# Splits held behind both halves of the rows, 64-row logits, and the last expert finished by output halves

## The chip, the cores and the metric

The kernel runs on one core of a Trainium2 chip. The metric is the time of one execution on the device in microseconds (us); three runs of the kernel before gave a median of 2085.16 (2085.03 to 2085.52). TensorE is the matrix engine, VectorE and ScalarE are the elementwise engines, GpSimd and SyncE mainly issue transfers here; in the profile they are PE (PEld for its weight loads), DVE, ACT, POOL and SP.

## The reference, cut to what matters

256 rows of 1024 numbers in fp32 go through two blocks. The first has two layers: adaptive norm, four kinds of attention side by side ("mix"), then a feed-forward part, dense in layer 0, eight experts with the best two of them per row in layer 1; a norm ends the block. The second block has a dense feed-forward, a mix of two attentions (16 heads of 64), and another dense feed-forward, each with a norm before and after.

```python
for l in range(2):                      # first block
    x = x + g_m * (mix(adaln(x)) @ w_out[l])
    h = adaln(x)
    f = swiglu(h, ...) if l == 0 else moe_swiglu(h, router, w1, w3, w2)
    x = x + g_f * f
x = rmsnorm(x, final_norm_g)
# second block
x = x + 0.5 * rmsnorm(swiglu(rmsnorm(x, pre1), g1, g3, g2), post1)
q, k, v = split(rmsnorm(x, premix) @ w_qkv)     # s = q k^T / 8 + bias, softmax, s v
x = x + rmsnorm(norms(o) @ w_out, postmix)
x = x + 0.5 * rmsnorm(swiglu(rmsnorm(x, pre2), h1, h3, h2), post2)
```

`swiglu(h, w1, w3, w2)` is `(silu(h @ w1) * (h @ w3)) @ w2`, 2816 wide in the dense layers and 3584 in an expert.

## The kernel before, in words

The 256 rows are two tiles of 128, t=0 and t=1. Every large product is made from operands split in two: a fast 32-bit form of the number (hi, xh) and the rest (lo, xl). `mm3` (lines 213 to 217) adds three products of one tile: xh·hi, xh·lo, xl·hi. So each megabyte of weights is loaded by a transfer that SyncE issues (`wload`), cast to hi by ScalarE (line 181) and reduced to lo by VectorE (line 185), both in `wsplit`. Up to 2048 columns are split by one instruction on each engine; in the first mix it is 1024. Four staging tiles and a few pairs of hi and lo (`stp`, `spl`, with extras for each stage) bound how far this runs ahead.

The code is written as a sequence, and a planner orders the instructions of each engine from it by its own costs, in the order of the program where several are ready; each engine then runs its list in order. `behind` adds an order between two instructions of one engine without a wait. One such order is at the seams: when a norm makes the transposed operand hT for t=0 (`norm_ev`, `scaled_hT`), the splits that follow are free for 2048 columns, and those of the next 3072 stand behind t=0's last hT instructions (`hold`, HELD_FROM and HELD). For t=1 there is none. In the second block the norms are deferred: hT is made from the raw x times a column gain, and the rows' scale r comes later from square sums and a Newton root of nine small VectorE instructions (`row_rstd`, `rsqrt`).

A dense layer (`dense_ffn`) has a first block of 256 columns and five of 512. A block makes two products per row tile, w1 and w3, in two halves of the contraction (kg); `gate` (ScalarE) and `value` (VectorE) combine them; the result is transposed and multiplied by w2 into four sums (fo), which have four of the eight banks of PSUM from the start. Block 0 takes the other four, two of `pps` and two of `hps`; later blocks use the two of `pps`.

The experts (`moe_pass`) run one after another on 128 gathered rows each; an expert has seven blocks of 512 columns, two sums (eo) and the products of w2 one block late (`down`). The results of the first seven go to memory and are gathered by row: `moe_combine` issues the gathers in the last expert's block 2, and its `add` (four VectorE instructions of 1024 columns for each t) runs behind block 5 for t=0 and block 6 for t=1. The last expert's own rows are put back by products with a one-hot matrix (`scatter`): split of a sum half, two products per t, a gated multiplication and an addition to x, for one half after the other. Then, for each t, eight transposes of x and their hT pieces, the square sums, the multiplication of x by its root and the final norm's gain, and again square sums, and after that the first dense layer of the second block.

The second block's mix (`mix2`) has four groups of four heads, and for each t a unit of four heads. Keys stand in a tile with zeros so that one product of 128 rows by 512 columns gives the logits of two heads (line 1478); GpSimd clears that tile and ScalarE copies the keys of each half of the partitions (line 566).

Of the kernel before, what the change touches and what calls it, by code (L numbers as in the profile page):

```python
# [41 lines left out]
HELD_FROM = 2048  # L42
HELD = 3072
# [52 lines left out]
def kernel(ctx: ExitStack, tc: tile.TileContext, a: dict, out: bass.AP):  # L96
# [76 lines left out]
    def wsplit(ld, pool=None, pre="", late=False, after=None, into=None, at=0):  # L173
# [3 lines left out]
        step = max(n for n in (1, 2, 4) if n * w <= wide["step"])  # L177
        for k in range(0, nk, step):
# [27 lines left out]
    hold = {"ops": None, "skip": 0}  # L206
# [77 lines left out]
    def norm_ev(t, y, ps, hT, gain, shift=None):  # L284
# [15 lines left out]
        if t == 0:  # L300
            hold.update(ops=ops, skip=HELD_FROM)

    def scaled_hT(t, hT, gain):
# [10 lines left out]
        if t == 0:  # L314
            hold.update(ops=ops, skip=HELD_FROM)
# [138 lines left out]
    def dense_ffn(hT, w1, w3, w2, post, hook=None, r=None):  # L454
        with ExitStack() as es:
# [5 lines left out]
            acc = [[aps(f"fo{t}{n}") for n in range(2)] for t in range(2)]  # L461
# [13 lines left out]
            for b in range(nb + 1):  # L475
                gT = [None, None]
                if b < nb:
# [22 lines left out]
                    if b == 0:  # L500
# [69 lines left out]
    def transpose_p(ap, pt, lg, idx, nk):  # L570
        nkc = nk // T
        per_bank = 4 // nkc
        for i0 in range(0, len(idx), per_bank):
            sub = idx[i0:i0 + per_bank]
            p = hps("ptr")
            for j, i in enumerate(sub):
                for kc in range(nkc):
# [3 lines left out]
                 p[:, :len(sub) * nk].rearrange("p (a b c) -> p a b c", a=len(sub), b=nkc))  # L581

# [402 lines left out]
    def moe_turn(mp, rnd, ps, oh, tp=None, xg=None):  # L985
# [6 lines left out]
        def step(i):  # L992
# [20 lines left out]
            ohT = (tp or mp).tile([T, 256], F32R, tag="ohT", name="ohT", bufs=2)  # L1013
# [12 lines left out]
    def moe_slots(pool, posm, yd):  # L1026
        sel, gate = rt["sel"], rt["gate"]
        zero = small([T, 9], I32, name="zslot", bufs=1)
        nc.vector.memset(zero, 0)
        tab = dram.tile([T * 9, 1], I32, name="slots")  # L1030
# [4 lines left out]
        for t in range(2):  # L1035
            ok = small([T, 8], name="pok")
            nc.vector.scalar_tensor_tensor(ok, posm[t], 128.0, sel[t], op0=ALU.is_le, op1=ALU.mult)
            v = small([T, 8], name="pv")
            nc.vector.scalar_tensor_tensor(v, posm[t], 8.0, erow, op0=ALU.mult, op1=ALU.add)
            nc.vector.tensor_tensor(v, v, ok, op=ALU.mult)  # L1040
# [9 lines left out]
            none = small([T, 2], name="pnone")  # L1050
            nc.vector.tensor_scalar(none, ab, 0.0, 1025.0, op0=ALU.is_equal, op1=ALU.mult)
            put = small([T, 2], I32, name="pput")
            nc.vector.scalar_tensor_tensor(put, ab, -1.0, none, op0=ALU.add, op1=ALU.add)
            for i in range(2):
                nc.gpsimd.indirect_dma_start(tab[:, :], bass.IndirectOffsetOnAxis(ap=put[:, i:i + 1], axis=0),
                                             tok[:, t:t + 1], None)
# [41 lines left out]
    def moe_pass(mp, gp, rnd, gate, posm, yh, yl, grow, ld_fn, split_fn, first=None, yd=None):  # L1098
# [47 lines left out]
        for e in range(NE):  # L1146
            xh, xl, ohT = nxt
            acc = [aps(f"eo{n}") for n in range(2)]
            for b in range(nb):
# [50 lines left out]
                if e == NE - 1 and b >= 5:  # L1200
                    behind(add.pop(0)(), m)
# [593 lines left out]
```

## Time and profile before

| What | us |
|---|---|
| median of three runs | 2085.16 |
| profiled execution | 2086.3 |
| its span, first to last instruction | 2084.5 |
| TensorE busy in the span | 2015.6 (97%) |
| VectorE busy | 1590.2 (76%) |
| ScalarE busy | 1251.4 (60%) |

The profile is of one execution. Matmuls overlap one another, so a busy TensorE means that one is under way, and the step from one start to the next is shorter than one's duration. The granted clock is 1.00 at 2.4 GHz and 0.50 at 1.2 GHz; a stretch's number is the mean over it. A row of the waits says who waited for what: total us, times, longest.

### The profile page before, as it was taken

To read this page: it belongs to the slowest core of one execution; us is meant where nothing else is said; L and a number is where in the kernel's file an instruction comes from. 1 tells how busy PE (TensorE), PEld (TensorE's weight loads), DVE (VectorE), ACT (ScalarE), POOL (GpSimd) and SP (SyncE) were. 2 spreads that over 40 slices of the span, in tenths; PEclk is the share of its full clock that TensorE was granted. 3 is DMA by queue.
4 is the path that set the end of the run, shared out by engine and by line. 5 is a ranking of instruction groups with operands and counts; after the bars stand their busy time and mean duration, and the time that the engine had idled before them with its cause. 6 is when DMAs were issued, how large, how long until landed. Compare 5 with 4: busy or idle time off the path is not lost.

```text
span 2084.5 us, 24737 instructions
## 1 busy us (share of the span) xinstructions
PE 2015.6 (97%) x9369; PEld 1623.0 (78%) x9370; DVE 1590.2 (76%) x2044; ACT 1251.4 (60%) x1469; POOL 37.1 (2%) x37
## 2 busy tenths in 40 slices
PE   7999999999899999999999999999989999998998
PEld 3867888777678888888888888888768886777886
DVE  6897878797688888888888888888895446556544
ACT  3766434476377777777777777777654345655442
POOL 0000000000000000000000000001000000000000
PEclk9999999999899999999999999999999999999999
DMA  8846876484499999999999999999966534436530
GB/s 331 292 177 256 353 292 242 173 233 150 154 340 379 366 369 374 385 380 382 379 386 379 378 378 378 383 363 399 396 243 240 185 101 163 165 135 228 202 122 20
DMA packets 89809, 586.38 MB, mean 281 GB/s; under 512 B 12880, under 2 KB 13776, under 8 KB 23376
## 3 DMA queue, kind: packets, MB, share of 16 engines
q1 hardware_dynamic: 81184, 566.05, 72.2%
q10 hardware_dynamic: 6432, 11.84, 1.6%
q0 software_dynamic: 2064, 6.83, 0.9%
q8 instruction: 75, 1.23, 0.2%
q14 instruction: 54, 0.44, 0.1%
HBM read 578.89 MB, written 5.78 MB: 280 GB/s over the span
## 4 chain that ended last, share of the span: by engine, by line
PE 67%; DVE 3%; ACT 1%; issue 1%; DVEq 0%; ACTq 0%
PE eh L215 10%; PE eh L216 10%; PE eh L214 10%; PE eo L215 5%; PE eo L216 5%; PE eo L214 5%; PE ff L214 4%; PE ff L215 4%; PE ff L216 4%; PE fo L214 2%; PE fo L215 2%; PE fo L216 2%; DVE lo L185 1%; PE egt L1129 1%; PE pj L216 1%
## 5 line engine op out<-in xcount | busy, mean ns | idle before, releaser
L185 DVE TENSOR_TENSOR lo<-st,hi 128x2048 fp32r<-128x2048 f32 (+2 forms) x327 | 648.1, 2002 | 138.2 <-ACT hi L181 131.2
L181 ACT CAST hi<-st 128x2048 fp32r<-128x2048 f32 (+2 forms) x328 | 540.2, 1681 | 156.9 <-PE ff L216 58.7
L185 DVE TENSOR_TENSOR lo<-sx,hi 128x2048 fp32r<-128x2048 f32 (+1 forms) x200 | 451.8, 2274 | 131.5 <-ACT hi L181 128.8
L181 ACT CAST hi<-sx 128x2048 fp32r<-128x2048 f32 (+1 forms) x200 | 374.5, 1899 | 136.5 <-PE ff L216 97.0
L214 PE MATMUL eh<-hi,xeh 128*128 128x512 f32 x896 | 351.4, 392 | 8.2 <-PEq L1415 5.1
L215 PE MATMUL eh<-lo,xeh 128*128 128x512 f32 x896 | 353.3, 394 | 2.4 <-DVE lo L185 2.4
L216 PE MATMUL eh<-hi,xel 128*128 128x512 f32 x896 | 350.4, 391 | 0.0
L214 PE MATMUL ff<-hi,hTh 128*128 128x512 f32 (+1 forms) x576 | 221.6, 385 | 10.5 <-DVE hTl L312 4.6
L215 PE MATMUL ff<-lo,hTh 128*128 128x512 f32 (+1 forms) x576 | 217.1, 377 | 1.5 <-DVE lo L185 1.5
L216 PE MATMUL ff<-hi,hTl 128*128 128x512 f32 (+1 forms) x576 | 217.4, 378 | 0.1
L214 PEld LDWEIGHTS eh<-hi,xeh 128*128 128x128 f32 x896 | 169.1, 189 | 45.2 <-ACTq L1415 5.5
L215 PEld LDWEIGHTS eh<-lo,xeh 128*128 128x128 f32 x896 | 169.2, 189 | 41.3 <-DVE lo L185 7.1
L216 PEld LDWEIGHTS eh<-hi,xel 128*128 128x128 f32 x896 | 169.2, 189 | 34.5
L215 PE MATMUL eo<-lo,egh 128*128 128x512 f32 x448 | 179.7, 401 | 0.3 <-DVE lo L185 0.3
L214 PE MATMUL eo<-hi,egh 128*128 128x512 f32 x448 | 175.2, 391 | 0.7 <-ACT egh L220 0.7
L216 PE MATMUL eo<-hi,egl 128*128 128x512 f32 x448 | 174.9, 390 | 0.5 <-DVE egl L220 0.5
L214 PEld LDWEIGHTS ff<-hi,hTh 128*128 128x128 f32 x576 | 111.5, 194 | 29.9 <-DVE hTl L312 4.8
L214 PE MATMUL pj<-hi,hTh 128*128 128x512 f32 (+3 forms) x320 | 123.9, 388 | 4.2 <-ACT hTh L220 3.1
L215 PEld LDWEIGHTS ff<-lo,hTh 128*128 128x128 f32 x576 | 111.5, 194 | 20.0 <-DVE lo L185 2.0
L216 PEld LDWEIGHTS ff<-hi,hTl 128*128 128x128 f32 x576 | 111.2, 193 | 20.1 <-DVE hTl L220 0.4
L216 PE MATMUL pj<-hi,hTl 128*128 128x512 f32 (+3 forms) x320 | 122.7, 384 | 3.4 <-DVE hTl L220 1.9
L215 PE MATMUL pj<-lo,hTh 128*128 128x512 f32 (+3 forms) x320 | 125.1, 391 | 0.9 <-DVE lo L185 0.8
(383 smaller groups left out, 2611.3 us busy)
## 6 DMA issues: line engine op xcount, KB each, us to landing
st<-in_e_dram SPq DMA_DIRECT2D x192, 1024.0 KB, 7.4
sx<-in_e_dram SPq DMA_DIRECT2D x144, 1024.0 KB, 7.6
st<-in_ada_dram SPq DMA_DIRECT2D x30, 1024.0 KB, 5.1
sx<-in_g_dram SPq DMA_DIRECT2D x19, 1024.0 KB, 6.0
sx<-in_h_dram SPq DMA_DIRECT2D x19, 1024.0 KB, 4.9
sx<-in_ada_dram SPq DMA_DIRECT2D x18, 1024.0 KB, 10.3
st<-in_w_in_dram SPq DMA_DIRECT2D x16, 1024.0 KB, 5.0
sx<-in_f_dram SPq DMA_DIRECT2D x15, 1024.0 KB, 7.0
```

Source lines behind the costliest of these rows:

```text
L181: c = nc.scalar.copy(hi[:, d], st[:, s])
L185: d = nc.vector.tensor_tensor(*rest.pop(), op=ALU.subtract)
L214: m = nc.tensor.matmul(ps, xh, wh, start=start, stop=False)
L215: nc.tensor.matmul(ps, xh, wl, start=False, stop=False)
L216: nc.tensor.matmul(ps, xl, wh, start=False, stop=stop)
L1129: nc.tensor.transpose(p[:, j * T:(j + 1) * T], g[:, j * T:(j + 1) * T], ident)
```

## The change

- `hold` becomes a list with a range for each t: splits whose first column counts 2048 to 5120 since t=0's hT stand behind t=0's last hT instructions, and those from 4096 to 8192 behind t=1's. Splits below 4096 have pieces of at most 1024 columns, and in `mix2` all have.
- `mix2` makes logits from keys without zeros: `row_logits` issues four products of 64 rows by 256 columns for a unit, on partitions 0 to 63 and 64 to 127 in turn, into two banks.
- The last expert ends with `finish_last`: products of sum half 0 for the last two blocks, then those of half 1, with half 0's split, scatter and additions (`back(0)`) before the last of these; `back(1)` is returned and called later. Its one-hot matrix is kept in another pool. The combine's adds stand behind blocks 4 and 5.
- The first dense layer of the second block gets a `start`: its block 0 runs by contraction halves, with four products' sums in the four banks `aps` (the fo sums take them afterwards). `start(h)` makes the hT pieces of half h for both t; `start(0)` then calls `back(1)`; both take square sums of x, multiply x by the final gain, and take square sums again; `start(2)` makes both roots for both t at once, and scales x.
- `moe_slots` uses a table of 16 instead of 9 numbers per partition, and drops the instruction that sent unused entries past its end.

```diff
-HELD_FROM = 2048
-HELD = 3072
+HELD = ((2048, 5120), (4096, 8192))
+FINE = 4096
...
-        step = max(n for n in (1, 2, 4) if n * w <= wide["step"])
+        step = max(n for n in (1, 2, 4) if n * w <= (1024 if hold["n"] < FINE else wide["step"]))
...
-            if hold["ops"] is not None:
-                if hold["skip"] <= 0:
-                    behind(c, hold["ops"][0])
-                    behind(d, hold["ops"][1])
-                hold["skip"] -= min(step, nk) * w
-                if hold["skip"] < -HELD:
-                    hold["ops"] = None
+            for first, last, ops in hold["ops"]:
+                if first <= hold["n"] < last:
+                    behind(c, ops[0])
+                    behind(d, ops[1])
+            hold["n"] += min(step, nk) * w
...
+    def scaled_half(t, h, hT, gain):
+        p = hps("trx")
+        for j in range(4):
+            nc.tensor.transpose(p[:, j * T:(j + 1) * T], halves(x[t])[h][:, j * T:(j + 1) * T], ident)
+        for j in range(4):
+            c, src = 4 * h + j, p[:, j * T:(j + 1) * T]
+            g = gain[:, c:c + 1]
+            nc.scalar.activation(hT[t][0][:, c, :], src, AF.Copy, scale=g)
+            nc.vector.scalar_tensor_tensor(hT[t][1][:, c, :], src, g, hT[t][0][:, c, :].bitcast(F32),
+                                           op0=ALU.mult, op1=ALU.subtract)
...
+                    if b == 0 and start is not None:
+                        lds = {(wi, kg): wload("f1", flat, kg) for kg in range(2) for wi, flat in enumerate((w1, w3))}
+                        p = {(t, wi): aps(f"ff{wi}{t}") for t in range(2) for wi in range(2)}
+                        for kg in range(2):
+                            start(kg)
+                            hl = pair()
+                            ws = [wsplit(lds[wi, kg], into=hl, at=wi * 4 * w) for wi in range(2)]
+                            for t in range(2):
+                                for wi in range(2):
+                                    up(p[t, wi], t, kg, ws[wi])
+                        start(2)
+                        for t in range(2):
+                            gate(t, p[t, 0])
+                            value(t, p[t, 1])
+                        acc = [[aps(f"fo{t}{n}") for n in range(2)] for t in range(2)]
...
+    def row_logits(bank, t, nk, qT, kT):
+        p = []
+
+        def f(h):
+            if not p:
+                p.extend(bank(f"lgr{i}") for i in range(2))
+                for k in range(4):
+                    hp, i = divmod(k, 2)
+                    r = slice(i * 64, (i + 1) * 64)
+                    nc.tensor.matmul(p[i][:, hp * nk:(hp + 1) * nk], qT[r, hp, t * T:(t + 1) * T],
+                                     kT[r, hp, :nk], start=True, stop=True)
+            hp, i = divmod(h, 2)
+            return p[i][:, hp * nk:(hp + 1) * nk]
+        return f
...
+        def finish_last(acc, ohT, gT, g):
+            def products(n, b, g):
+                ws = split_fn(ld_fn("e2", "e2", 2 * b + n, NE - 1))
+                for k in range(4):
+                    mm3(acc[n], g[0][:, k * T:(k + 1) * T], g[1][:, k * T:(k + 1) * T], *ws[k],
+                        False, b == nb - 1 and k == 3)
+
+            def back(n):
+                sl = slice(n * 512, n * 512 + 512)
+                e = wk.tile([T, D], F32R, tag="y", name="eys", bufs=2)
+                split_to(halves(e)[0], halves(e)[1], acc[n])
+                for t in range(2):
+                    p = (pps if n else hps)("sct")
+                    for i in range(2):
+                        nc.tensor.matmul(p, ohT[:, t * T:(t + 1) * T], halves(e)[i], start=i == 0, stop=i == 1)
+                    nc.vector.scalar_tensor_tensor(p, p, gate[t][:, NE - 1:NE], grow[:, sl], op0=ALU.mult, op1=ALU.mult)
+                    nc.vector.tensor_tensor(x[t][:, sl], p, x[t][:, sl], op=ALU.add)
+
+            products(0, nb - 2, gT)
+            g = transposes(g)
+            products(0, nb - 1, g)
+            products(1, nb - 2, gT)
+            back(0)
+            products(1, nb - 1, g)
+            return lambda: back(1)
...
-                if e == NE - 1 and b >= 5:
+                if e == NE - 1 and b >= 4:
                     behind(add.pop(0)(), m)
...
-            widen(ap, MIX_PAIRS[1])
+            widen(ap, MIX_PAIRS[1], 1024)
...
-                kb = ap.tile([T, 2, 2, 256], F32, tag="k2", name="k2", bufs=2)
-                nc.gpsimd.memset(kb, 0.0)
+                kb = ap.tile([T, 2, 256], F32, tag="k2", name="k2", bufs=2)
...
-                    for g in range(2):
-                        evac(kb[g * 64:(g + 1) * 64, :, g, t * T:(t + 1) * T], p4[g * 64:(g + 1) * 64, 2:4, :])
+                    evac(kb[:, :, t * T:(t + 1) * T], p4[:, 2:4, :])
...
-    for t in range(2):
-        scaled_hT(t, hT, fgain)
-        r = row_rstd(t, "x")
-        for n in range(2):
-            xs = halves(x[t])[n]
-            nc.vector.scalar_tensor_tensor(xs, xs, r, halves(fin)[n], op0=ALU.mult, op1=ALU.mult)
-        q = row_rstd(t, "q")
-        nc.vector.tensor_tensor(q, q, r, op=ALU.mult)
-        r1.append(q)
+    def start1(h):
+        if h < 2:
+            for t in range(2):
+                scaled_half(t, h, hT, fgain)
+            if h == 0:
+                rest()
+            for t in range(2):
+                xs = halves(x[t])[h]
+                for i in range(2):
+                    if i:
+                        nc.vector.tensor_tensor(xs, xs, halves(fin)[h], op=ALU.mult)
+                    jk = wk.tile([T, 512], BF16, tag="junk", name="junk", bufs=2)
+                    nc.scalar.activation(jk, xs, AF.Square, accum_out=fsum[:, 2 * i + h, t:t + 1])
+            return
...
+        for t in range(2):
+            r1.append(s[10][:, t:t + 1])
+            nc.vector.tensor_scalar(x[t], x[t], s[5][:, t:t + 1], None, op0=ALU.mult)
```

## Rows read from the trace of the kernel before

**Rows 1.** The page's first part: busy us, share of the span, instructions.
```profile
PE 2015.6 (97%) x9369; PEld 1623.0 (78%) x9370; DVE 1590.2 (76%) x2044; ACT 1251.4 (60%) x1469; POOL 37.1 (2%) x37
```
**Rows 2.** Busy time by stretch: PE, PEld, DVE, ACT, POOL, clock, DMA share, GB/s.
```profile
700.00:1430.00 730.00, 730.00 (x3316) 601.10 (x3315) 639.53 (x357) 531.29 (x372) 9.20 (x5) 1.00 0.98 378
1480.00:1500.00 20.00, 20.00 (x92) 16.55 (x91) 17.04 (x10) 15.22 (x11) 0.00 (x0) 1.00 1.00 406
1500.00:1520.00 20.00, 17.57 (x77) 13.71 (x76) 19.09 (x13) 11.68 (x9) 0.00 (x0) 1.00 0.77 269
1520.00:1562.00 42.00, 33.11 (x172) 27.07 (x171) 38.42 (x80) 23.74 (x45) 0.00 (x0) 0.88 0.67 252
1735.00:1757.00 22.00, 17.72 (x73) 12.51 (x71) 18.78 (x53) 16.67 (x33) 0.00 (x0) 0.92 0.56 203
1757.00:1880.00 123.00, 121.88 (x622) 94.72 (x621) 66.74 (x161) 72.21 (x160) 1.90 (x2) 1.00 0.47 165
1878.00:1903.00 25.00, 19.27 (x120) 17.42 (x119) 18.95 (x53) 18.32 (x35) 0.00 (x0) 0.86 0.58 231
```
**Rows 3.** Who TensorE waited for: us in total, times, longest.
```profile
PE ff L214 <- DVE hTl L312: 4.6, 1, 4.6
...
PE ff L214 <- ACT hTh L220: 3.1, 1, 3.1
...
PE eh L215 <- DVE lo L185: 2.4, 3, 1.8
PE ff L214 <- ACT s L483: 2.3, 1, 2.3
...
PE sct L1112 <- DVE x L1116: 2.0, 1, 2.0
...
PE trx L307 <- DVE x L1116: 1.7, 1, 1.7
PE pj L216 <- DVE hTl L312: 1.6, 1, 1.6
...
PE sct L1112 <- ACT eyh L220: 0.7, 1, 0.7
```
**Rows 4.** Busy time of the combine's (DVE, POOL) and the scatter's (PE, PEld, DVE) instructions.
```profile
1499.00:1530.00 31.00, 8.93 (x8) 0.00 (x0) 1.00 0.59 204
...
1530.00:1542.00 12.00, 3.63 (x8) 1.65 (x8) 5.21 (x8) 0.82 0.57 201
```
**Rows 5.** The last dense layer's start in order of time, then a stretch (as rows 2).
```profile
1887.49 2.29 DVE L185 TENSOR_TENSOR lo<-sx,hi 128x2048 fp32r<-128x2048 f32 x1
...
1890.20 2.29 DVE L185 TENSOR_TENSOR lo<-sx,hi 128x2048 fp32r<-128x2048 f32 x1
...
1893.19 0.61 DVE L312 SCALAR_TENSOR_TENSOR hTl<-trx,cols,hTh 128x128 fp32r<-128x128 f32 x2 [0.18 <-ACT hTh L311]
...
1896.09 0.15 DVE L246 SCALAR_TENSOR_TENSOR rsq<-rsq 128x1 f32<-128x1 f32 x1
...
1897.42 0.16 DVE L238 SCALAR_TENSOR_TENSOR rsq<-rsq 128x1 f32<-128x1 f32 x1
...
1893.59:1899.50 5.91, 5.91 (x27) 5.91 (x28) 3.26 (x20) 4.41 (x12) 0.00 (x0) 0.50 0.67 277
```
**Rows 6.** The second mixing layer's start in order of time, VectorE and ScalarE.
```profile
1743.26 2.29 DVE L185 TENSOR_TENSOR lo<-st,hi 128x2048 fp32r<-128x2048 f32 x1
...
1749.01 2.28 DVE L185 TENSOR_TENSOR lo<-st,hi 128x2048 fp32r<-128x2048 f32 x1
...
1756.35 0.68 ACT L1463 ACTIVATE n<-pj,rsk 128x512 f32<-128x512 f32 x1
```
**Rows 7.** Logits: the group of line 1478, then two of line 675 by time.
```profile
L1478 PE MATMUL lg<-k,q 128*128 128x512 f32 x32 | 15.6, 608 | 0.4 <-ACT k L566 0.3
...
152.06 1.02 PE L675 MATMUL lgp<-kbc,qTc 128*128 128x512 f32 x2
...
140.41 1.10 PE L675 MATMUL lgp<-kbc,qTc 128*128 128x256 f32 x4
```

More of the change, by code (lines that the diff above doesn't have):

```diff
@@ L460, in dense_ffn @@
             es.callback(stages, None)
-            acc = [[aps(f"fo{t}{n}") for n in range(2)] for t in range(2)]
+            if start is None:
+                acc = [[aps(f"fo{t}{n}") for n in range(2)] for t in range(2)]
             nb = len(FF_BLOCKS)
@@ L1027, in moe_slots @@
         sel, gate = rt["sel"], rt["gate"]
-        zero = small([T, 9], I32, name="zslot", bufs=1)
+        zero = small([T, 2 * NE], I32, name="zslot", bufs=1)
         nc.vector.memset(zero, 0)
-        tab = dram.tile([T * 9, 1], I32, name="slots")
+        tab = dram.tile([T * 2 * NE, 1], I32, name="slots")
         nc.gpsimd.dma_start(tab.rearrange("(p f) o -> p (f o)", p=T), zero)
@@ L1049, in moe_slots @@
             ab = two("pab")
[L1050 to L1051 removed]
             put = small([T, 2], I32, name="pput")
[L1053 removed]
+            nc.vector.tensor_scalar(put, ab, -1.0, 0.0, op0=ALU.add, op1=ALU.max)
             for i in range(2):
@@ L1056, in moe_slots @@
                                              tok[:, t:t + 1], None)
+            ok = small([T, 8], name="pok")
+            nc.vector.scalar_tensor_tensor(ok, posm[t], 128.0, sel[t], op0=ALU.is_le, op1=ALU.mult)
             nc.vector.tensor_tensor(ok, ok, enot, op=ALU.mult)
@@ L1170, in moe_pass @@
                         nc.vector.tensor_tensor(g, s, p, op=ALU.mult)
+                if rnd == 0 and e == NE - 1 and b == nb - 1:
+                    return finish_last(acc, ohT, gT, g)
                 if prev is not None:
@@ L1432, in moe @@
                 widen(mp, MOE_PAIRS)
-                moe_pass(mp, mo, 0, gate, posm, yh, yl, grow, load,
+                rest = moe_pass(mp, mo, 0, gate, posm, yh, yl, grow, load,
                          lambda ld: ld if isinstance(ld, list) else wsplit(ld, after=end.pop() and (rt["mm"], rt["mm"]) if end else None),
@@ L1437, in moe @@
                 widen()
+        return rest
     def mix2(hT, r, then):
@@ L1589 @@
             if not t:
[L1590 removed]
+                begin["op"] = hold["ops"][0][2][0]
     def chain(*fs):
@@ L1631 @@
     mix1(1, h_m1[0], feed([(1, 3), router_setup, (1, 5)], MIX1_ADA), lambda t, acc: rt.update(acc=acc) if t else route0(acc))
-    moe()
+    rest = moe()
     fin = load_row(ROW_FIN)
@@ L1649, with root @@
     hT, r1 = hT_tiles(), []
-    for t in range(2):
-        scaled_hT(t, hT, fgain)
-        r = row_rstd(t, "x")
-        for n in range(2):
-            xs = halves(x[t])[n]
-            nc.vector.scalar_tensor_tensor(xs, xs, r, halves(fin)[n], op0=ALU.mult, op1=ALU.mult)
-        q = row_rstd(t, "q")
-        nc.vector.tensor_tensor(q, q, r, op=ALU.mult)
-        r1.append(q)
+    fsum = sml.tile([T, 12, 2], F32, name="fsum")
+    def start1(h):
[12 more added lines that the diff above has]
+            return
+        s = [fsum[:, i, :] for i in range(12)]
+        tt = nc.vector.tensor_tensor
+        def root(v, r):
+            nc.vector.tensor_scalar(v, v, D * EPS, None, op0=ALU.add)
+            rsqrt(v, s[6], s[7], s[8], r, math.sqrt(D))
+        tt(s[4], s[0], s[1], op=ALU.add)
+        root(s[4], s[5])
+        tt(s[9], s[2], s[3], op=ALU.add)
+        tt(s[9], s[9], s[5], op=ALU.mult)
+        tt(s[9], s[9], s[5], op=ALU.mult)
+        root(s[9], s[10])
+        tt(s[10], s[10], s[5], op=ALU.mult)
+        for t in range(2):
+            r1.append(s[10][:, t:t + 1])
+            nc.vector.tensor_scalar(x[t], x[t], s[5][:, t:t + 1], None, op0=ALU.mult)
     norm_mx, h_mx, r_mx = deferred(col("premix"), "k")
     norm_f2, h_f2, r_f2 = deferred(col("pre2"), "q")
-    dense_ffn(hT, a["g1"], a["g3"], a["g2"], chain(normed_residual(load_row(ROW_P1), 0.5), norm_mx), r=r1)
+    dense_ffn(hT, a["g1"], a["g3"], a["g2"], chain(normed_residual(load_row(ROW_P1), 0.5), norm_mx), r=r1, start=start1)
     mix2(h_mx, r_mx, norm_f2)
```

39 lines of the change are left out of this document (16 added, 23 removed).

## The prediction

> **What bounds the kernel now.** I read the page's first part, then busy time by stretch, then who TensorE waited for, then the instructions in order of time at the places where it waited. TensorE is busy 2015.6 of 2084.5 us [rows 1]: only its own work or its idle time can shorten the run, and other engines count where TensorE waits for them. By stretch [rows 2], the experts' middle has TensorE busy all of its 730 us at full clock (730 / 3316 records = 0.22 us each), and the second mixing layer 121.9 of 123; there only less TensorE work counts. The losses stand at seams: 1500 to 1562 (the last expert into the next dense layer) has 62.0 - 17.57 - 33.11 = 11.3 us idle, and a mean granted clock of 0.88 in its longer part; 1735 to 1757 (into the second mixing layer) 4.3 us idle at 0.92; 1878 to 1903 (into the last dense layer) 5.7 us at 0.86. At the first, VectorE is nearly full: 19.09 of 20 and 38.42 of 42. The waits [rows 3] name the same places: 4.6 for a late hTl at the last seam and 1.6 at the one before, 2.4 for lo beside the combine, 2.0 and 1.7 for x at the scatter, 2.3 for a gate's s.
>
> **Last dense layer (orders).** The second half of the rows (t=1) has its hTl pieces between two splits of the next weight block: VectorE runs lo of 2.29 us at 1887.49 and again at 1890.20, and the last pair of hTl starts at 1893.19; TensorE takes up at 1893.59, and then makes 27 records in 5.91 us at a granted clock of 0.50 [rows 5]. The change puts the splits of elements 4096 to 8192 behind t=1's last piece. Both 2.29 leave the chain: hTl is done 4.6 earlier, near 1889.2, about when t=0's products end (the wait of 4.6 before 1893.59 began at 1889.0). So the 4.6 goes, and if the clock stays up, half of the 5.91 (3.0) too: 7.6. What is late next: rsq, done at 1897.58, comes at 1893.0, and TensorE, 48 products of 256 columns later (0.11 each, 5.3 us), wants the next block at about 1894.5; its moved split of 2.29 can follow rsq, at 1895.3 or somewhat later. I take 7.6 less 1.1 for that wait and 1.5 for a clock that still dips: **-5**, bounds -8 and 0 (the splits are wanted at once, and the wait only moves).
>
> **Second mixing layer (orders and finer splits).** The same pattern: lo of 2.29 at 1743.26, for which TensorE waits, and another at 1749.01 ahead of t=1's last hTl [rows 6]. In pieces of 1024 the first can start TensorE 1.1 us sooner; the other leaves the chain (2.3). The limit behind it is the row scale: the first product's evacuation waits for it until 1756.35, and as its squares follow the last hTh it comes 2.3 sooner too, a little more with the 1.1. **-3**, bounds -6 (the idle time of the stretch and its slow clock) and 0. Cutting this layer's 16 splits in two costs one more start each on engines that are busy 66.74 and 72.21 of 123 us [rows 2]: nothing.
>
> At the other seams the same orders bring nothing: there TensorE waits 3.1 for t=0's hTh [rows 3], which no weight split stands ahead of in either version. The slot table's arithmetic precedes a gather wanted only by the next expert: nothing.
>
> **Row products.** 16 products of 128 rows by 512 columns are 32 records [rows 7]. Two in a row of such a form take 1.02 us, and the last of them some 0.6 (the mean of one is 608 ns), so one begins per 0.43: 32 x 0.43 = 13.8 us. The new form has 32 products of 64 rows by 256 columns, 64 records; one of 256 columns costs half, 0.215, or by the row of four, of which the last takes some 0.4, (1.10 - 0.4) / 3 = 0.23. One after another: 64 x 0.215 = 13.8, or 14.9. Whether two halves of the rows overlap no row shows. If they pair wholly, half: -6.9. The records of every row start in order, so in a unit of four products the second record of one could run with the first of the next: five steps instead of eight, 8 units x 5 x 0.215 = 8.6, -5.2. A switch between 128 and 64 rows drains at worst what a record takes beyond its step, 0.6 - 0.43 = 0.17, 16 times: +2.7. Bounds -6.9 and +1.1 + 2.7 = +3.8. I take -5.2 with two thirds of the drains: **-3.5**. TensorE is full in this layer, so this reaches the end undiminished. One copy of k less, and one memset less, stand on engines with room: nothing.
> The Trainium skill's TensorEngine Tiling (Array Packing), section Key Properties, says that tiles of the array load weights and multiply in parallel, but that a change of tiling mode drains TensorE. No run here shows either yet; by its first half alone the term would be -5.2, by its second up to 2.7 less.
>
> **Experts' end into the dense layer.** Before, the combine (8.93 us of VectorE in 31 [rows 4]) runs in the last two blocks on a full engine. TensorE waits 2.4 for lo, 0.7 for the scatter's first split, 2.0 and 1.7 for x, 2.3 for s [rows 3]. The change moves each half of the combine a block earlier: its first half, 4.47, goes into a stretch where VectorE had 20 - 17.04 = 2.96 free [rows 2], so 1.5 spills and may stall TensorE by up to the 2.4 that it costs now. The sum's half 0 is finished first: its scatter, adds and transposes of half of x lie beside 12 or 24 products of half 1 (2.6 or 5.3 us), and half 1's chain beside the first half of block 0, 48 products of 256 columns (5.3). A half's chain: split 1.3, products 3.63 / 2 = 1.8, gated adds 5.21 / 2 = 2.6 [rows 4], eight transposes, counted as 256-column products, 0.9, and a first pair of hT pieces 0.6 [rows 5]: 7.2. So 1.9 stays open twice, 3.8. The gates then wait for both roots, some 28 small steps in a row after the last square; nine took 1.5 us (1896.09 to 1897.58 [rows 5]), so 4.7. Block 0 sits in the sums' four banks, so 24 products of the next block in the other two (5.3) cover that, and the 2.3 for s goes.
> Waits gone: 0.7 + 2.0 + 1.7 + 2.3 = 6.7, less the 3.8 that stay open: 2.9. The clock: 0.12 of 42 us is 5.0 lost, 4.0 of it while busy; with idle times of 2 instead of a row of them I count it as won: **-6.5** (rounded down from 6.9).
> VectorE's own limit: the norm gain and root take four operations of 512 columns and two of 1024 where four did both, at most 4 x 0.65 = 2.6 more. It could win its idle 0.91 + 3.58, the 4.47 moved out and one split not yet due, 2.3, less 2.6: 8.7, so -6.5 fits. Bounds -11 (all idle time) and +5 (the spilled combine stalls 2.4 more and the 2.6 is all late).
>
> **Sum.** -5 - 3 - 3.5 - 6.5 = -18. The profiled execution took 2086.3 us (span 2084.5 and 1.8 around it), so 2068.3; it lies 1.1 above the median of the runs, 2085.16, which makes **2067.2**.
>
> **The rivals.**
> *A. Row products do not overlap and drain.* For: no row shows an overlap, and records start in order. Against: the halves use other rows and other banks. +3.8 for -3.5: 2074.5. Chance 0.17.
> *B. The waits at the two later seams move.* The held splits come late, after squares on ScalarE and roots on VectorE. For: TensorE needs the next split and a bank freed by a row scale. Against: both come 2.3 to 4.6 earlier than before. Those two terms are nothing: 2075.2. Chance 0.12.
> *C. All goes well.* No seam has a slow clock and the rows pair wholly: 7 more, 2060. Chance 0.07.
> *D. The other side: VectorE's queue at the experts' end.* It was busy 57.5 of 62 us there; two chains now follow one another, with more work. If it lags at the first, TensorE idles before block 0 and again at its second half, and the lag carries the held splits of the later seams' pattern into this one: +5, and +2.7 for the drains without a gain from rows, nothing at the other seams: some 2093. It decides from where VectorE has no gap up to the first 512-column product of that dense layer and TensorE idles there over 11 us. Chance 0.05.
> *E. It does not do what it says*: the instructions' planned order stays, the moved adds trade places: 2085. Chance 0.04.
>
> **How the numbers follow.** The forecast, 2061 to 2073, has 0.55; the rest is above. A to C lie in 2058 to 2079, which is the range: it leaves out D, E and the tails of B and C, under 0.2. Within 0.2% (4.2 us) is about what a measurement here cannot tell from no change. Faster 0.88 (the forecast, C, nearly all of A and B), the same 0.06 (E, tails of B), slower 0.06 (D, tails of A).
>
> **What would show it.** Right: lo stalls in the blocks with the combine, but no wait of over 2 us at the scatter or for s; TensorE's wait for hTl at the last seam under 1 us, and that layer's first 512-column product some 5 us nearer to its start; 64-row records that start in pairs, their mean step well under 0.2 us. Wrong: 64-row records 0.215 or more apart; a granted clock below 0.9 still at all three seams; VectorE without a gap from 1483 to the dense layer.

## The result and the profile after

The changed kernel takes 2065.44 us (median of 4 runs, 2063.29 to 2069.5) where the one before took 2085.34 beside it: a ratio of 0.9904, 95% interval 0.9887 to 0.9921, or 19.9 us. The forecast was 2067.2. The profiled execution took 2065.45 with a span of 2063.7.

The page's first part, of after (busy us, share of the span, instructions), against [rows 1]:

```profile
PE 2002.4 (97%) x9402; PEld 1616.4 (78%) x9402; DVE 1589.7 (77%) x2049; ACT 1251.0 (61%) x1477; POOL 36.2 (2%) x33
```

TensorE is busy 13.2 us less, of 20.8 us of span: the larger part of the gain is busy time (half clock and the row products), the rest idle time. Busy time by stretch, of after, against [rows 2] (columns as there):

```profile
700.00:1430.00 730.00, 730.00 (x3316) 601.07 (x3315) 639.62 (x357) 531.45 (x372) 9.21 (x5) 1.00 0.98 378
1480.00:1500.00 20.00, 17.56 (x77) 13.65 (x77) 18.72 (x12) 11.68 (x9) 0.00 (x0) 1.00 0.90 349
1500.00:1520.00 20.00, 18.04 (x80) 14.23 (x79) 19.25 (x13) 14.29 (x10) 0.00 (x0) 1.00 0.83 304
1520.00:1557.00 37.00, 34.74 (x205) 30.17 (x204) 34.66 (x51) 24.95 (x45) 0.00 (x0) 1.00 0.69 276
1557.00:1575.00 18.00, 15.55 (x70) 12.49 (x69) 10.45 (x30) 8.55 (x10) 0.00 (x0) 1.00 0.89 370
1728.00:1750.00 22.00, 20.36 (x96) 15.49 (x95) 18.50 (x55) 17.14 (x39) 0.00 (x0) 1.00 0.41 130
1750.00:1866.00 116.00, 115.20 (x637) 92.66 (x635) 68.53 (x176) 70.68 (x163) 0.00 (x0) 1.00 0.53 189
1863.00:1881.00 18.00, 16.56 (x116) 14.39 (x115) 15.12 (x50) 14.52 (x33) 0.00 (x0) 1.00 0.59 231
```

The granted clock is 1.00 at all three seams, where it was 0.88, 0.92 and 0.86. New is the second row: TensorE, full from 1480 to 1500 before, now stands still for 2.4 us there. The waits of after, against [rows 3] (us, times, longest):

```profile
PE eh L218 <- DVE lo L185: 4.0, 3, 1.8
...
PE ff L217 <- ACT hTh L223: 3.1, 1, 3.1
PE pj L217 <- ACT hTh L223: 3.1, 1, 3.1
PE ff L217 <- ACT s L496: 2.5, 1, 2.5
...
PE trx L320 <- DVE x L461: 1.9, 3, 1.5
...
PE ff L219 <- DVE hTl L313: 1.8, 2, 1.2
...
PE ff L217 <- DVE hTl L325: 0.3, 1, 0.3
```

The 4.6 for hTl is 0.3, the scatter's waits are gone, the two of 3.1 are as before; lo has grown from 2.4 to 4.0, and the 2.3 for s, which I said would go, is 2.5.

Where the time went is best seen between fixed points of TensorE's work. The table has the distances between starts of its records, read from each trace: first expert product to the last sum of the dense layer behind the experts; from there to the last o product (the second mixing layer); from there to the last 256-column product of the last dense layer (the last seam); from there to the last product of w2 (the rest). In the same table is the ratio to the kernel before with its interval.

```
kernel                       experts+dense   mix2   seam   rest   ratio [95%]
before                          1168.42     141.55  22.55  174.46
after                           1162.02     133.27  15.85  174.93  0.9904 [0.9887, 0.9921]
e1 rows alone                   1168.36     138.90  22.33  174.46  0.9995 [0.9986, 1.0004]
e2 orders alone                 1165.84     136.46  15.84  174.91  0.9935 [0.9922, 0.9949]
e3 no orders                    1161.02     138.95  22.51  174.46  0.9958 [0.9944, 0.9971]
e4 rows in other order          1162.03     134.09  15.83  174.97  0.9908 [0.9893, 0.9923]
e5 whole splits                 1161.68     135.44  15.84  174.95  0.9912 [0.9890, 0.9935]
e6 combine spread               1161.51     133.27  15.84  174.95  0.9906 [0.9889, 0.9922]
e7 roots first                  1159.70     133.16  15.84  174.91  0.9896 [0.9879, 0.9912]
e8 both                         1158.37     133.47  15.84  174.92  0.9884 [0.9867, 0.9900]
e9 pieces, no hold for t=1      1161.23     138.05  21.42  174.46  0.9941 [0.9921, 0.9961]
e10 combine partly on ScalarE   1158.11     133.48  15.85  174.92  0.9874 [0.9854, 0.9894]
e11 half the combine left out   1161.41     133.64  15.85  174.95  0.9898 [0.9877, 0.9918]
e12 combine partly on GpSimd    1160.99     133.54  15.83  174.91  0.9883 [0.9863, 0.9903]
```

What lies ahead of the first expert product is not in it: it ends anywhere from 565.7 to 570.8 us in these traces, without order. Seam and rest repeat within 0.2 us in kernels that do not differ there, mix2 within some 0.5 (133.2 to 133.6 in after, e6 to e8 and e10 to e12). The first column holds the first expert, which takes from 120.6 to 122.0 us, also without order (its waits for hi are 3.1 in before's list, 4.3 in after's, 2.7 and 4.2 in e3's and e2's). Counted from the second expert's first product, the column repeats much better: 1047.6 in before and e1; 1044.1 in e2; 1040.3 to 1040.6 in after, e3, e4, e5, e6, e9 and e11; 1038.1 in e7; 1036.5 in e8; 1037.1 in e10; 1039.0 in e12. Small effects are read from these distances; the ratios alone would not show them.

### The profile page after: what moved, and what is told of

The parts are those of the page before. It is cut to its first block, busy times and chain, and to the rows that moved or that the text cites. A ratio compares the mean times of both kernels' runs of the same rounds, so it can differ in the third digit from the quotient of the medians.

```text
span 2063.7 us, 24799 instructions
## 1 busy us (share of the span) xinstructions
PE 2002.4 (97%) x9402; PEld 1616.4 (78%) x9402; DVE 1589.7 (77%) x2049; ACT 1251.0 (61%) x1477; POOL 36.2 (2%) x33
## 4 chain that ended last, share of the span: by engine, by line
PE 68%; DVE 2%; ACT 1%; issue 1%; DMA 1%; SPq 0%; DVEq 0%; ACTq 0%
PE eh L218 10%; PE eh L219 10%; PE eh L217 10%; PE eo L218 5%; PE eo L217 5%; PE eo L219 5%; PE ff L219 4%; PE ff L218 4%; PE ff L217 4%; PE fo L217 2%; PE fo L218 2%; PE fo L219 2%; DVE lo L185 1%; PE egt L1171 1%; PE pj L218 1%; PE pj L219 1%
## 5 line engine op out<-in xcount | busy, mean ns | idle before, releaser
L219 PE MATMUL ff<-hi,hTl 128*128 128x512 f32 (+1 forms) x576 | 212.7, 374 | 2.3 <-DVE hTl L313 1.8
```

Of the source, the lines that this page charges most:

```text
L219: nc.tensor.matmul(ps, xl, wh, start=False, stop=stop)
```

## The experiments

**Each part alone.** e1 has of the change only `row_logits`, with its tile of keys; e2 only the two held ranges and the pieces of 1024; e3 is after without these (the main lines):

```diff
-HELD = ((2048, 5120), (4096, 8192))
+HELD_FROM = 2048
+HELD = 3072                        # t=0 alone, as before
-        step = max(n for n in (1, 2, 4) if n * w <= (1024 if hold["n"] < FINE else wide["step"]))
+        step = max(n for n in (1, 2, 4) if n * w <= wide["step"])
-            widen(ap, MIX_PAIRS[1], 1024)
+            widen(ap, MIX_PAIRS[1])
```

> The kernel before with the row products alone. Theory (whole pairing, a price at each switch): in the trace of after the 64-row records start in pairs 0.006 to 0.007 us apart, a pair every 0.209 us, so four steps a unit, and each switch costs about 0.3 us (0.1 on the record before, 0.1 on the first pair, 0.1 at the exit); summed from start to start its records take 10.2 us where the 128-row form took 13.5. So -3.3 us against before, and all of it between the first pj product and the last o product of the second mixing layer. Rival (my prediction's working): five steps of eight and two thirds of sixteen drains of 0.17 us, -3.5, which is the same sum by another split: told apart by the pair step and the record before a switch, not by the time. Rival A (no overlap, drains): +3.8. The total alone can't tell -3.3 from nothing with certainty; the stretch in the trace can.

Measured: -2.65 in the second mixing layer and nothing elsewhere; the time, 2083.35, is not told apart from before, as expected of so small a part. The -2.65 is not the products' price alone. Summed from start to start, their records take 9.3 us where they took 13.5. The half clock at that seam (0.92 over 22 us before, 1.8 us lost) is gone too, and in its place TensorE waits for n; before's list has no such wait. The stretch of [rows 2], of e1, and the wait:

```profile
1735.00:1757.00 22.00, 16.45 (x70) 11.56 (x69) 19.16 (x50) 17.54 (x31) 0.00 (x0) 1.00 0.56 204
```
```profile
PE pj L214 <- ACT n L1478: 1.4, 1, 1.4
```

> The kernel before with the two held ranges and the 1024-element splits alone. Theory: the orders give what the traces of before and after show at the two later seams: last o product to the last 256-column product of the last dense layer 22.5 us before, 15.8 in after, -6.7; and first pj to last o of the second mixing layer -8.3 in after, less 3.3 for the rows, -5.0; together -11.7, a time near 2073.6. The prediction had -8 (2077). Rival: part of the second mixing layer's gain came from how the dense layer before it ended in after (its shortened experts' end), so the orders alone give -6.7 and about -3 there: 2075.6. Rival B (waits move): no change, 2085.

Measured: 2070.69. The last seam gives -6.7 and the mixing layer -5.1, as the theory had it. Unforeseen, the dense layer behind the experts gains too, in its old form: experts+dense is 2.6 shorter (3.5 behind the last expert, less the first expert's wait), and e2's list of waits no longer has the 2.3 for s, while the mean clock from 1520 to 1562 is 0.92 where it was 0.88 (1.7 us). The "other seams" of my prediction are not nothing.

> The kernel after with the orders and the finer splits undone: rows and the experts' end remain. Theory (the parts add): 3.3 for the rows and 6.4 for the experts' end with its dense layer (first expert product to the last sum of that dense layer is 6.4 us shorter in after than in before): -9.7, a time near 2075.6, with half-clock stretches back at the two later seams. Rival (the parts lean on each other): the dense layer's start in block 0 needs its held splits, so without the orders the experts' end gives 3 or less: 2079 or more.

Measured: 2075.74, the theory's time. The half clock is back at the last seam only (0.86 from 1867 to 1892); at the one into the second mixing layer it is 1.00, as in e1. Against e1 (rows alone) the experts' end gives -7.3. Against e2, where the orders have already won at that place, the same code gives only -3.8: the parts do not add there.

**What pairs the row products.** e4 issues the two products of the lower rows first, then the two of the upper:

```diff
-                for k in range(4):
+                for k in (0, 2, 1, 3):
```

> The kernel after with the four 64-row products of a unit in another order: both of the lower 64 rows first, then both of the upper ones. Theory (records start in order, and only a record that stands right behind one of the other half can run beside it): eight records of a unit take seven steps instead of four, 3 x 0.209 x 8 units = 5.0 us more than after. Rival (the halves queue independently, each record starts when its rows are free): the four of the lower half run beside the four of the upper one, no change against after.

Measured: next to no loss (2065.94; mix2 +0.8, not +5.0). TensorE's rows by time, of after and then of e4 (start, us, what, count; the stretch of a group is that of all its records):

```profile
1758.10 0.40 PE L217 MATMUL pj<-hi,hTh 128*128 128x512 f32 x1
1758.44 0.49 PE L620 MATMUL lgr<-k,q 64*128 64x256 f32 x2
...
1758.44 2.00 PE L620 MATMUL lgr<-k,q 64*128 64x256 f32 x16
1760.36 0.50 PE L218 MATMUL pj<-lo,hTh 128*128 128x512 f32 x1
```
```profile
1758.72 0.40 PE L217 MATMUL pj<-hi,hTh 128*128 128x512 f32 x1
1759.06 0.49 PE L620 MATMUL lgr<-k,q 64*128 64x256 f32 x2
...
1759.06 2.10 PE L620 MATMUL lgr<-k,q 64*128 64x256 f32 x16
1761.09 0.49 PE L218 MATMUL pj<-lo,hTh 128*128 128x512 f32 x1
```

The second line of each, a look at the first 0.02 us, has two records under way within 0.49 us, and one alone takes 0.48: they run side by side. In after 16 records, two units, fill 1.92 us up to the next product; at one per 0.215 they would fill 3.4. In e4 the program has two records of each of two products of the lower half ahead of any of the upper, and they pair nevertheless, 2.03 us for 16. So the halves take their records independently in both orders that were run, and my rule that records of all rows start in order falls. The Trainium skill, TensorEngine Tiling (Array Packing), section Key Properties, says that tiles operate independently: this trace agrees.

**The pieces and the hold.** e5 takes the pieces of 1024 out (the last two pairs of lines of e3's diff); e9 keeps them and holds nothing behind t=1:

```diff
-        hold["ops"].append((*HELD[t], ops))
+        if t == 0:
+            hold["ops"].append((*HELD[0], ops))
```

> The kernel after with whole splits (2048 elements) again, the two held ranges stay. Theory (my prediction's working): in the second mixing layer the pieces of 1024 start TensorE 1.1 us sooner and the hold of t=1 brings the rest, so first pj to last o grows from 133.3 to 134.4 us, the last seam (15.85 us from the last o to the last 256-column product) stays, and the run is 1.1 longer. Rival 1 (the pieces carry the seam): they account for the gain beyond my 3 us there (5.1 to 5.7 measured), so that stretch grows by 2 or more. Rival 2 (the pieces are idle): no change there, and the 0.45 us that the rest of the last dense layer took longer in every kernel with the orders goes.

> The kernel after with the second held range (t=1's) taken out: the pieces of 1024 and t=0's range stay. Theory (my prediction's step for the last seam, and what the run with whole splits left over at the other): all of the gain from the last o to the last 256-column product, 6.7 us, is that range's, so 15.85 goes back to 22.5; and of the 5.7 us of the second mixing layer the pieces have 2.2, so first pj to last o grows from 133.3 by the remaining 3.5: in all some 10 us slower than after. Rival: the pieces alone already let t=1's hTl through between two halves of a split, so part of the gain stays, some 3 us at each of the two places.

Measured: without the pieces mix2 is 2.2 longer, with waits for lo (1.5) and for a late lg (1.1) in e5's list, so rival 1 holds; the seam does not need them. Without the hold both places fall back, mix2 by 4.8 and the seam by 5.6 of its 6.7, and its wait is there again (waits of e9):

```profile
PE ff L218 <- DVE hTl L326: 4.6, 1, 4.6
...
PE pj L218 <- ACT n L1535: 2.4, 1, 2.4
```

Against e3, which has neither, the hold alone is worth 138.95 - 135.44 = 3.5 in mix2, the pieces alone 138.95 - 138.05 = 0.9, not much above the scatter of that column, and both 5.7. Alone the pieces bring TensorE earlier to a late root (the 2.4 for n, 1.4 in e3's list), and behind that wait stands half clock, which e3 has not there (e9):

```profile
1735.00:1757.00 22.00, 18.98 (x75) 14.41 (x75) 16.05 (x38) 15.25 (x28) 0.00 (x0) 0.92 0.73 263
```

That is 22 x 0.08 = 1.8 us of what the pieces win beside the hold. At the seam they keep 1.1 of the gain without the hold, with the same wait of 4.6 as in e3 and a clock of 0.93 (1866 to 1891) for 0.86. The hold costs 0.47 in the rest of the last dense layer: the moved split is not yet there when TensorE starts the next block at 1880.23, and its first product with lo starts 0.54 behind the one before it, where 0.23 is usual (after):

```profile
1878.42 2.29 DVE L185 TENSOR_TENSOR lo<-sx,hi 128x2048 fp32r<-128x2048 f32 x1
```
```profile
1880.23 0.49 PE L217 MATMUL ff<-hi,hTh 128*128 128x512 f32 x1
1880.77 0.50 PE L218 MATMUL ff<-lo,hTh 128*128 128x512 f32 x1
```

I had allowed 1.1 for that wait.

**The two waits that after has and I had not forecast.** The combine on VectorE, of after, in its first block (by time):

```profile
1488.08 2.29 DVE L185 TENSOR_TENSOR lo<-st,hi 128x2048 fp32r<-128x2048 f32 x1
1490.28 1.22 DVE L1135 TENSOR_TENSOR ycomb<-ycomb,row 128x1024 f32<-128x1024 f32 x1
1491.41 0.69 DVE L223 TENSOR_TENSOR egl<-egt,egh 128x512 fp32r<-128x512 f32 x1
1492.01 1.22 DVE L1136 TENSOR_TENSOR x<-x,ycomb 128x1024 f32<-128x1024 f32 x1
1493.14 6.69 DVE L185 TENSOR_TENSOR lo<-st,hi 128x2048 fp32r<-128x2048 f32 x3
...
1557.89 0.16 DVE L1735 TENSOR_TENSOR fsum<-fsum 128x2 f32<-128x2 f32 x1
1557.96 0.75 DVE L1741 TENSOR_SCALAR x<-x,fsum 128x1024 f32<-128x1024 f32 x1
1558.63 0.15 DVE L1736 TENSOR_TENSOR fsum<-fsum 128x2 f32<-128x2 f32 x1
1558.70 0.75 DVE L1741 TENSOR_SCALAR x<-x,fsum 128x1024 f32<-128x1024 f32 x1
1559.36 0.16 DVE L1729 TENSOR_SCALAR fsum<-fsum 128x2 f32<-128x2 f32 x1
1559.43 2.28 DVE L185 TENSOR_TENSOR lo<-sx,hi 128x2048 fp32r<-128x2048 f32 x1
1561.63 0.16 DVE L226 TENSOR_SCALAR fsum<-fsum 128x2 int32<-128x2 int32 x1
1561.70 1.22 DVE L185 TENSOR_TENSOR lo<-sx,hi 128x1024 fp32r<-128x1024 f32 x1
1562.84 0.15 DVE L232 TENSOR_TENSOR fsum<-fsum 128x2 f32<-128x2 f32 x1
...
1564.20 0.16 DVE L1738 TENSOR_TENSOR fsum<-fsum 128x2 f32<-128x2 f32 x1
```

Above, VectorE goes from one thing to the next without a gap, and the split at 1493.14 is the one TensorE waits for (the step between its records is 1.97 longer than the usual 0.22 there, and 1.99 longer in the next block). Below are the roots: small steps (fsum), and between two of them whatever large piece was ready. The chain takes from 1553.58 to 1564.36.

e6 puts the combine's eight operations one behind each half block of blocks 3 to 6; e7 puts the w3 splits of the second block and the scaling of x behind the roots; e8 has both.

```diff
 # e6
-                if e == NE - 1 and b >= 4:
-                    behind(add.pop(0)(), m)         # four operations at once
+                    if rnd == 0 and e == NE - 1 and b >= 3:   # in the loop over e1, e3
+                        behind(add.pop(0)(), m)     # one operation
 # e7
+            if rooted is not None:                  # in wsplit; b == 1, w3
+                behind(d, rooted)
-            nc.vector.tensor_scalar(x[t], x[t], s[5][:, t:t + 1], None, op0=ALU.mult)
+            behind(nc.vector.tensor_scalar(x[t], x[t], s[5][:, t:t + 1], None, op0=ALU.mult), end)
```

> The kernel after with the combine's eight VectorE operations one behind each half block of the last expert's blocks 3 to 6, instead of four behind each of blocks 4 and 5. Theory (VectorE's queue): four operations of 4.47 us in one block of 16.8 us overrun the 2 to 3 us that VectorE has free in a block, so lo comes late and TensorE waits 2.9 us in the first such block and 2.3 in the second; two operations of 2.2 us a block fit, and 4 of these 5.2 us go: first to last expert product from 953.7 to some 950, the run 3 to 4 us shorter. Rival (the stall belongs to the gathered rows or the shared memory, not to the queue): the waits for lo stay near 4 us in sum wherever the operations stand. A second rival: the last two operations, now in block 6, make x late for the first scatter and add as much at the experts' end.

Measured: the theory and its second rival both. From the first to the last product of the experts' first two matrices it is 4.2 shorter (953.72 to 949.56; 3.5 from the second expert on), and from there to the dense layer's end 3.65 longer. 1.9 of that is a new wait for lo in block 6 (1.7 idle, and the longer step of the record ahead); the rest is clock, in a stretch behind the wait for s (e6):

```profile
PE eo L218 <- DVE lo L185: 3.6, 4, 1.7
...
PE ff L217 <- ACT s L496: 2.5, 1, 2.5
```
```profile
1560.00:1575.00 15.00, 12.55 (x51) 9.87 (x50) 6.00 (x13) 5.69 (x8) 0.00 (x0) 0.89 0.64 267
```

The same wait of 2.5 is followed by full clock in after, 1.00 over the same 15 us, and here by a mean of 0.89: 15 x 0.11 = 1.65.

> The kernel after with the small steps of both roots ahead of the second block's w3 splits and of the scaling of x. Theory (VectorE's queue again): in after the roots' chain runs from 1553.58 to 1564.3 us with 2.2, 2.28 and 1.22 us of splits and 1.34 us of scaling of x between its steps, while TensorE can do only the 48 products of the second block's first matrix until the gates free its banks; with the splits behind, the roots end near 1557.5, the gates free the banks before TensorE asks, and its wait of 2.6 us for s at 1563.4 goes: last expert product to the end of that dense layer from 208.3 to 205.7 us. Rival (the wait moves): the w3 splits, 2.29 us each and now behind roots, scaling and gates, are late by as much; 208 stays, with a wait for lo in place of that for s.

Measured: as the theory had it. The chain runs from 1552.82 to 1557.26 and no wait for s is in e7's list; -2.3. VectorE, of e7, at its end:

```profile
1556.90 0.16 DVE L243 SCALAR_TENSOR_TENSOR fsum<-fsum 128x2 f32<-128x2 f32 x1
1557.10 0.16 DVE L1741 TENSOR_TENSOR fsum<-fsum 128x2 f32<-128x2 f32 x1
1557.18 1.41 DVE L1744 TENSOR_SCALAR x<-x,fsum 128x1024 f32<-128x1024 f32 x2
```

> The kernel after with both: the combine's operations spread and the roots' steps first. If both theories hold and add, 3.5 + 2.6 = 6 us less than after, near 2059. If they share a cause later on (the scatter or x late), less than the larger of the two gains is added by the other.

Measured: -3.65 in experts+dense, 2061.04 us. With the wait for s gone the clock stays up (1.00 from 1550 to 1575), and the spread combine is worth 1.6 from the second expert on (1038.1 to 1036.5); the 1.9 in block 6 remains.

e10 to e12 change the combine again, e10 and e12 on top of e7:

```diff
 # e10: first operation of a half; the other six behind the half blocks of blocks 3 to 5
-            f = nc.vector.tensor_scalar(g[0], g[0], w[:, 0:1], None, op0=ALU.mult)
+                nc.scalar.activation(g[0], g[0], AF.Copy, scale=w[:, 0:1])
 # e11
-                if e == NE - 1 and b >= 4:
+                if e == NE - 1 and b >= 5:
 # e12: as e10 but for the places of the operations, and
-            nc.vector.tensor_tensor(g[0], g[0], grow, op=ALU.mult)
+                nc.gpsimd.tensor_tensor(g[0], g[0], grow, op=ALU.mult)
```

> The kernel after with the roots' steps first, the combine's first operation of each half of the rows on ScalarE, and its other six on VectorE, one behind each half block of the last expert's blocks 3 to 5, so that none is left in block 6. Theory (VectorE's queue, and block 6 has no room since its own chain ends there): the wait of 1.9 us in block 6, which came with two operations there, goes, and those of 0.8 stay: first expert product to the end of that dense layer from 1159.7 us (roots first alone; 1158.4 with eight operations over four blocks) to some 1156.5. Rival (2.5 us of VectorE a block is too much for the 2.4 it has free): waits for lo of 2 us come back in blocks 4 and 5, and it stays at 1158 or more.

Measured: 1158.11, no better than e8, and 0.6 longer than it from the second expert on. In block 6 a wait of 0.6 is left of the 1.9, and two of 0.7 stayed, much as expected; but ScalarE's scaling now delays a split's other half (waits of e10):

```profile
PE eo L220 <- DVE lo L185: 2.1, 3, 0.7
...
PE eo L219 <- ACT hi L181: 1.3, 1, 1.3
```

> The kernel after with the combine's two halves back behind blocks 5 and 6 of the last expert, where the kernel before has them; all else as after. Theory (block 6 has no room): the second half's 4.47 us of VectorE now runs among the split of the sum and the first scatter; x is late for the first row transposes, and what the experts' stretch wins (2.3 of its waits) comes back larger after it: first expert product to the end of that dense layer from 1162.0 to 1164 or more. Rival (only the number of full blocks counts): the stall has the same size in whichever block, 1162.0 within 0.7.

In this form the last block returns ahead of the line that issues its operations, so the second half of the combine (t=1) is left out, and the question is not answered. What it tells: the half that is left stalls TensorE as before (a gap of 1.97 in its block), and experts+dense is no shorter than after's from the second expert on (1040.3 for 1040.4), because what is won (2.6) ahead of the wait for s is lost behind it to a stretch at 0.89, as in e6. Whether the combine belongs in the late blocks stays open.

> The kernel after with the roots' steps first, and the combine on three engines: the first scaling on ScalarE, the product with the output row on GpSimd, and only two operations a half (1.28 and 1.22 us) on VectorE, one behind a half block of blocks 3 to 5. Theory (VectorE's queue alone makes the stalls): VectorE has 1.28, 2.5 and 1.22 us of the combine in three blocks that have some 2.4 free each, so the waits for lo shrink to those that stand there anyway (0.7 and 0.8 at the experts' end): first expert product to the end of that dense layer from 1158.1 us (the best so far) to some 1156, and the run 1 to 3 us under it. Rival (the two engines block each other): a GpSimd operation that reads two tensors of SBUF holds up the splits on VectorE, which read two as well; then splits of 2.29 us stand in the trace with over 3 us beside the GpSimd operation, lo is late there, and the stretch stays at 1158 or grows by what the GpSimd operations last. The rule for the rival is in the Trainium skill, SBUF — State Buffer, section SBUF: two separate sides: the pair of ports that VectorE and GpSimd share is a lock for a whole instruction.

Measured: 1160.99, 2.9 worse than e10, of which 1.0 is the first expert's and 1.9 the last one's; the rival holds. GpSimd and VectorE by time, and the waits, of e12:

```profile
1463.69 2.41 POOL L1137 TENSOR_TENSOR ycomb<-ycomb,row 128x1024 f32<-128x1024 f32 x1 [19.48 <-DVE ycomb L1136]
...
1483.32 4.38 POOL L1137 TENSOR_TENSOR ycomb<-ycomb,row 128x1024 f32<-128x1024 f32 x1 [17.22 <-DVE ycomb L1136]
...
1485.36 4.50 DVE L185 TENSOR_TENSOR lo<-sx,hi 128x2048 fp32r<-128x2048 f32 x1
```
```profile
PE eo L220 <- DVE lo L185: 3.2, 4, 1.4
```

Nearly alone (VectorE works on nothing from 1463.6 to 1465.9), the product takes 2.41. The second starts 0.16 behind a split, takes 2.0 more, as long as that split lasts, and the split after it takes 4.50 for 2.29: first the one stands still, then the other. So 2.2 us of VectorE were lost to save 1.22, and TensorE's longest wait for lo, 1.4, ends at 1489.92, when that split is done. The page named in the expectation, the Trainium skill's SBUF — State Buffer, section SBUF: two separate sides, says that whichever engine starts first has the shared pair of ports for the whole instruction and the other fully blocks; these numbers agree.

The best kernels here are e8 and e10, 0.9884 and 0.9874 of before. Both intervals overlap that of after, and each other; that the two are faster than after rests on experts+dense, 3.9 and 3.3 us shorter from the second expert on.

## Why the prediction was right, and which steps failed

The sum was -18; the fixed points give -20.9 (-6.4, -8.3, -6.7 and +0.5). That the time is so near is in part luck: inside the terms for the row products and the experts' end errors offset one another. The terms, by the prediction's own steps:

- **Last dense layer, -5.** -6.7, less 0.5 for the moved split, is -6.2. "So the 4.6 goes" held, and e9 shows that the hold for t=1 does it. "1.5 for a clock that still dips" failed: the clock is 1.00. The root, forecast 13.7 us after the last o product (1893.0 less 1879.35), is done 14.1 after it (1878.32 less 1864.21).
- **Second mixing layer, -3.** -5.1 alone. The mechanism was right, both sizes short: the hold 3.5 for 2.3, the pieces 2.2 beside it for 1.1. I counted the two splits and left the clock out, which was 0.92 there and is 1.00 with the orders alone (e2). On top of the rows, which have 1.00 there already (e1, e3), the 5.6 is all waits, among them hTl 1.6, n 1.4, lg 0.6 and lo 0.8.
- **Row products, -3.5.** -2.65 alone, with the clock and the wait for n changed beside it; -3.2 beside the orders, where the clock is 1.00 with and without the rows. The size came out by errors that cancel. "Five steps instead of eight" failed: four. "Two thirds of the drains" of 0.17 failed the other way: by the record starts a change of mode costs about 0.1 on the record before it, 0.1 on the first pair and 0.1 at the exit, 0.3 for each stretch of 64-row records. And I had not foreseen that other products stand inside three of the eight units: after has 10 such stretches, and some records run alone.
- **Experts' end, -6.5.** -6.4, or -7.2 without the first expert, and again from other parts than I gave. The clock (4.0) came as forecast; the scatter's waits went; of "3.8 that stay open" 2.1 are there, as waits for hTl with their gaps. But "24 products of the next block cover that, and the 2.3 for s goes" failed. The cover was even larger, 48 products of w1; the chain of small steps was 10.8 us long instead of 4.7, since the planner puts splits of 2.29, 2.28 and 1.22 and two scalings of 0.75 between its steps (e7: 4.4 without them). And the combine, which I valued at nothing within a bound of 2.4, costs 2.5 from the first to the last of the experts' products (e3 against e1): both halves now stall TensorE there, where the second fell into the idle time of the old end.
- **"At the other seams the same orders bring nothing"** failed for the dense layer behind the experts in its old form (e2). The sum did not suffer, since that form is gone; but the experts' end is worth only 3.8 on top of the orders.

None of the rivals' times came about. A is excluded by the pairs, B by e2, E by the time. D's sign (VectorE without a gap from 1483) came in part: VectorE has 1.28 and 0.75 us free in the two stretches of 20 us, and its queue costs TensorE there, but it does not lag at the seam. Of C's two conditions, no slow clock came about, and whole pairs in five of eight units; its 2060 did not, since the combine (2.5) and the roots (2.5) took back what they gave: e8 and e10, with both mended in part, take 2061.04 and 2060.75.

## What to carry to other kernels

Where an engine prepares operands for the bound engine, put the short pieces that finish a stage ahead of the long pieces for the next one, at every seam: here that order, with not one instruction less, was two thirds of the gain (e2: 13.9 of 20.9 us). A chain of small steps whose end somebody waits for needs the same care, since each step lets one long piece in. Work that is moved into a block of some 17 us, of which the full engine has some 2 free (the experts' middle: 639.6 of 730 busy), has to come in portions that fit, and moving it to GpSimd beside a full VectorE did not help here (e12), because the two took turns.

## What the hardware showed that I had not expected

- Products on the lower and the upper 64 rows run in pairs in both program orders that were tried: a pair of records of 256 columns in 0.21 us, where a record of 128 rows by 512 takes 0.43.
- Elementwise work of GpSimd and VectorE on SBUF, both with two tensor inputs, alternates instead of overlapping, in the one place of e12 where they meet: 4.38 for 2.41 and 4.50 for 2.29.
- The same wait of TensorE (2.5 us for s) is followed by a full clock in after and e3, and by 0.89 in e6 and e11. The same waits at the seam into the second mixing layer (0.8 for lo, 1.6 for hTl) are followed by half clock in before (a mean of 0.92) and by 1.00 in e1 and e3. Why stays open: no run here varies what stands ahead of the wait alone.
